# More loads issued in halves, and one more group whose late partitions go HBM to HBM, in a rank-and-scatter kernel

## The chip, the cores and the metric

One core of a Trainium2 chip. The metric is the device time of one launch in microseconds (us), as the median of several runs. All ratios below use runs in the fast state; where a kernel was run once, its state is unknown and I say "one run". The profile is of one further execution; its span runs from the first to the last instruction and is about 2 us under the device time. Where I quote from the trace what no view prints (single DMA packets, single increments of a semaphore), I say so.

## The reference

```python
def reference(x, scores):            # x: 8 x 2048 x 2560 fp32, scores: 8 x 2048 fp32
    order = np.argsort(scores, axis=1)
    ranks = np.argsort(order, axis=1)
    out = np.zeros_like(x)
    out[np.arange(B)[:, None], ranks, :] = x
    return out
```

Each row of x (10,240 bytes) moves to the place that the rank of its score names. 168 MB are read and 168 MB written; the arithmetic is small.

## The kernel before

VectorE counts, for each score, how many of its batch are smaller. The rows are moved in two ways at once:

- Groups of 256 rows are loaded into SBUF by GpSimd (the first group's load by SP, on queue 1) and scattered by two indirect DMAs of 128 rows each (58 such groups, 8 buffers). This is queue 0.
- One group of each of the first six batches, and single rows left out of scatters, go straight from HBM to HBM, one DMA a row, issued by SP (queue 1) and ACT (queue 10). I call these direct rows.

Some loads are issued as two halves. For some groups the scatter leaves out four partitions, by making their rank too large for the bounds check; these 8 rows go as direct rows. In the trace's packet records each of the 14,792 rows scattered is one packet of 10,240 bytes, and each of the 56 left out one of 4 bytes.

```python
THIN = [(b, 4) for b in range(1, B)]        # groups whose scatters skip ...
HOLES = range(48, 48 + 4)                   # ... these partitions
HALVED = range(20)                          # loads issued in two halves
...
def load(line, k, sem):
    ...
    for j in range(m if k in HALVED else 1):
        part = slice(j * D, (j + 1) * D) if k in HALVED else slice(0, m * D)
        line.eng.dma_start(out=xb[k % NBUF][:, part], in_=rows[:, part]).then_inc(sem, 16)
...
# GpSimd, for each group k
if k >= LAG and k + NBUF - LAG < len(BULK):
    scatters_done(pl, k - LAG)              # a buffer comes free
    load_ahead(k + NBUF - LAG)
pl.wait(*loaded[k])
for j in range(GROUPS[g][1]):
    scatter(k, j)                           # bounds_check=N - 1 where (b, g) in THIN
...
nc.gpsimd.drain()
for k in range(max(0, len(BULK) - NBUF), len(BULK)):
    scatters_done(sp, k)                    # SP waits for the last scatters
```

SP waits for all direct rows.

## Time and profile before

| | before |
|---|---|
| device time, median | 778.43 us (778.36 to 778.47) |
| span of the profiled execution | 777.4 us |

The lines are in the prediction.

### The profile page before, as it was taken

To read this page: it belongs to the slowest core of one execution; us is meant where nothing else is said; L and a number is where in the kernel's file an instruction comes from. 1 tells how busy PE (TensorE), PEld (TensorE's weight loads), DVE (VectorE), ACT (ScalarE), POOL (GpSimd) and SP (SyncE) were. 2 spreads that over 40 slices of the span, in tenths; PEclk is the share of its full clock that TensorE was granted. 3 is DMA by queue.
4 is the path that set the end of the run, shared out by engine and by line. 5 is a ranking of instruction groups with operands and counts; after the bars stand their busy time and mean duration, and the time that the engine had idled before them with its cause. 6 is when DMAs were issued, how large, how long until landed. Compare 5 with 4: busy or idle time off the path is not lost.

```text
span 777.4 us, 8189 instructions
## 1 busy us (share of the span) xinstructions
PE 34.6 (4%) x170; PEld 29.9 (4%) x170; DVE 400.0 (51%) x825; ACT 0.0 (0%) x1; POOL 157.4 (20%) x201
## 2 busy tenths in 40 slices
PE   4000010020020020120000000000000000000000
PEld 4000010010010010120000000000000000000000
DVE  5999989979979979889999200000000000000000
ACT  0000000000000000000000000000000000000000
POOL 4114223212112121212121212121211112121000
PEclk9655555555555555565555555555555555555555
DMA  8999999999999999999999999999999999999995
GB/s 358 420 418 420 411 418 414 418 421 415 417 416 419 421 414 424 417 423 416 425 418 423 418 423 418 421 420 422 419 423 419 423 418 423 418 422 419 420 414 188
DMA packets 78914, 320.15 MB, mean 412 GB/s; under 512 B 28640, under 2 KB 54112, under 8 KB 54112
## 3 DMA queue, kind: packets, MB, share of 16 engines
q0 software_dynamic: 27648, 300.90, 91.2%
q1 hardware_dynamic: 25904, 10.93, 5.4%
q10 hardware_dynamic: 25344, 8.16, 4.2%
q14 instruction: 17, 0.14, 0.0%
q8 instruction: 1, 0.02, 0.0%
HBM read 168.41 MB, written 168.35 MB: 433 GB/s over the span
## 4 chain that ended last, share of the span: by engine, by line
DMA 44%; DVE 36%; another core or an unknown queue 5%; issue 4%; PE 3%; POOL 3%; POOLq 0%; SPq 0%
DMA out_dram<-x,rank_i 38%; DVE trash L238 34%; DMA x<-in_x_dram 6%; PE ps_all L196 2%; POOL out_dram L422 2%; DVE s_all L339 2%; POOL x L126 1%; PE ps_row L298 0%; DMA s_in<-in_scores_dram 0%; PE ps_col L175 0%; DVE rank L270 0%; DVE rank_i L276 0%; DVE rank L264 0%; POOLq L446 0%
## 5 line engine op out<-in xcount | busy, mean ns | idle before, releaser
L238 DVE TENSOR_SCALAR_CACHE_REDUCE trash<-s_all,s_col 128x1792 bf16<-128x1792 f32 (+7 forms) x240 | 315.1, 1348 | 4.6
L422 POOL DMA_INDIRECT out_dram<-x,rank_i x116 | 113.0, 974 | 141.5 <-DMA x<-in_x_dram 36.5
L126 POOL DMA_DIRECT2D x<-in_x_dram x76 | 42.6, 563 | 441.8 <-DMA out_dram<-x,rank_i 411.1
L238 DVE SCALAR_TENSOR_TENSOR trash<-s_all,s_col,mask 128x256 bf16<-128x256 f32 x128 | 61.6, 481 | 0.0
L196 PE MATMUL ps_all<-ident,s_col 128*128 128x128 f32 x128 | 27.9, 408 | 3.1 <-DVE s_all L339 2.8
L196 PEld LDWEIGHTS ps_all<-ident,s_col 128*128 128x128 f32 x128 | 26.3, 221 | 4.1 <-DVE s_all L339 3.1
L298 PE MATMUL ps_row<-ident,rank 128*1 128x128 f32 x26 | 6.7, 354 | 392.5 <-DVE rank_i L284 335.2
L339 DVE COPY s_all<-ps_all 128x512 f32<-128x512 f32 x32 | 20.1, 684 | 1.7 <-PE ps_all L196 1.4
L238 DVE DVE_READ_ACCUMULATOR trash<-s_all,s_col 128x1 f32 x240 | 19.7, 82 | 0.0
L298 PEld LDWEIGHTS ps_row<-ident,rank 128*1 128x1 f32 x26 | 1.7, 90 | 395.7 <-DVE rank_i L284 337.4
L238 DVE DVE_READ_ACCUMULATOR trash<-s_all,s_col,mask 128x1 f32 x128 | 10.6, 83 | 0.0
L309 DVE TENSOR_SCALAR thin_i<-ps_row 1x8 int32<-1x8 f32 x7 | 1.1, 154 | 16.7 <-PE ps_row L298 16.7
L324 DVE TENSOR_SCALAR rows_i<-ps_row 1x256 int32<-1x256 f32 x6 | 2.5, 412 | 4.1 <-PE ps_row L298 4.1
L183 DVE COPY s_col<-ps_col 128x128 f32<-128x128 f32 x1 | 0.3, 292 | 4.5 <-PE ps_col L175 4.5
L175 PE MATMUL ps_col<-ident,s_in 8*128 8x8 f32 x16 | 2.1, 264 | 3.7 <-DMA s_in<-in_scores_dram 3.7
L276 DVE CAST rank_i<-rank 128x16 int32<-128x16 f32 (+3 forms) x11 | 2.0, 179 | 0.4
L270 DVE TENSOR_TENSOR rank<-rank,acc 128x16 f32<-128x16 f32 (+3 forms) x11 | 2.0, 178 | 0.4
L175 PEld LDWEIGHTS ps_col<-ident,s_in 8*128 8x128 f32 x16 | 2.0, 211 | 3.7 <-DMA s_in<-in_scores_dram 3.7
L264 DVE TENSOR_TENSOR rank<-acc,acc 128x16 f32<-128x16 f32 (+3 forms) x11 | 1.9, 170 | 0.4
L284 DVE TENSOR_SCALAR rank_i<-rank,hole 128x2 int32<-128x2 f32 x7 | 1.6, 228 | 0.2
L156 POOL TENSOR_SCALAR_AFFINE_SELECT mask<-mask 128x256 f32<-128x256 f32 x2 | 0.8, 402 | 0.0
L168 DVE MEMSET acc<- 128x128 f32 x1 | 0.2, 165 | 1.1 <-SPq L102 1.1
(10 smaller groups left out, 1.8 us busy)
## 6 DMA issues: line engine op xcount, KB each, us to landing
x<-in_x_dram POOLq DMA_DIRECT2D x38, 2560.0 KB
x<-in_x_dram POOLq DMA_DIRECT2D x38, 1280.0 KB
out_dram<-in_x_dram SPq DMA_DIRECT2D x800, 10.0 KB
out_dram<-in_x_dram ACTq DMA_DIRECT2D x792, 10.0 KB
x<-in_x_dram SPq DMA_DIRECT2D x2, 1280.0 KB, 8.6
out_dram<-x,rank_i POOLq DMA_INDIRECT x116, 47.7
s_in<-in_scores_dram SPq DMA_DIRECT2D x1, 64.0 KB
```

Source lines behind the costliest of these rows:

```text
L126: line.eng.dma_start(out=xb[k % NBUF][:, part], in_=rows[:, part]).then_inc(sem, 16)
L175: nc.tensor.transpose(out=ps_col[:, B * c:B * (c + 1)], in_=s_in[:, r + j:r + m * P:m], identity=ident[:B, :B],)
L196: nc.tensor.transpose(out=ps_all[:, P * c:P * (c + 1)], in_=s_col[:, c, b:b + 1].to_broadcast([P, P]), identity=ident[:],)
L238: do(out=trash[i][:, :P * (hi_c - lo_c)], in0=s_all[:, P * lo_c:P * hi_c], accum_out=acc[i][:, col:col + 1], **how,)
L264: nc.vector.tensor_tensor(out=rank[:, cols], in0=acc[0][:, cols], in1=acc[1][:, cols], op=OP.add)
L270: nc.vector.tensor_tensor(out=rank[:, cols], in0=rank[:, cols], in1=acc[2][:, cols], op=OP.add)
L276: nc.vector.tensor_copy(out=rank_i[:, cols], in_=rank[:, cols])
L284: nc.vector.tensor_scalar(out=rank_i[:, cols], in0=rank[:, cols], scalar1=hole[:], scalar2=None, op0=OP.add,)
L298: nc.tensor.transpose(out=ps_row[:1, P * j:P * (j + 1)], in_=rank[:, col:col + 1], identity=ident[:],)
L324: nc.vector.tensor_scalar(out=rows_i[b][:].rearrange("o (p j) -> o p j", p=P), in0=ps_row[:1, :WIDE].rearrange("o (j p) -> o p j", p=P), s ...
L339: nc.vector.tensor_copy(out=s_all[:, 512 * q:512 * (q + 1)], in_=ps_all[:, 512 * q:512 * (q + 1)],)
L422: nc.gpsimd.indirect_dma_start(out=out_flat, out_offset=bass.IndirectOffsetOnAxis(ap=rank_i[:, col:col + 1], axis=0), in_=xb[k % NBUF][:, ...
```

## The change

Two things: the halved loads go from k = 0..19 to k = 0..31, so that queue 0 gives more turns to the direct rows; and group (7, 5) skips partitions 44-47, meant for another late DMA engine, 5.3 us behind the median at the last scatter. By turns I mean packets served: in the trace of the kernel before an engine serves, on average, 41.5 packets of each of the three queues from 480 to 500 us, where loads are whole and direct rows are waiting, and 54.3 of queue 0 from 120 to 140 us, where loads are halved.

```diff
-    THIN = [(b, 4) for b in range(1, B)]
-    HOLES = range(48, 48 + 4)
+    THIN = {**{(b, 4): 48 for b in range(1, B)}, (7, 5): 44}
+    HOLES = sorted(set(THIN.values()))
 
-    HALVED = range(20)
+    HALVED = range(32)
 ...
-    hole = pool.tile([P, 1], F32, name="hole")
+    hole = pool.tile([P, len(HOLES)], F32, name="hole")
 ...   (one mask per hole, and each use picks its own)
-                row = b * N + r + HOLES[i % 4] * m + i // 4
+                row = b * N + r + (THIN[b, g] + i % 4) * m + i // 4
```

More of the change, by code (lines that the diff above doesn't have):

```diff
@@ L209 @@
         bc = broadcast(0)
-        dve.did(
-            nc.vector.tensor_reduce(
-                out=hole[:],
-                in_=ident[:, HOLES[0]:HOLES[0] + 4],
-                axis=mybir.AxisListType.X,
-                op=OP.add,
+        for i, first in enumerate(HOLES):
+            dve.did(
+                nc.vector.tensor_reduce(
+                    out=hole[:, i:i + 1],
+                    in_=ident[:, first:first + 4],
+                    axis=mybir.AxisListType.X,
+                    op=OP.add,
+                )
             )
-        )
         dve.after(dve, dve.n)
@@ L281, in ranks @@
                     cols = slice(b * C + first_col(g), b * C + first_col(g + 1))
+                    i = HOLES.index(THIN[b, g])
                     dve.after(dve, dve.n)
@@ L286, in ranks @@
                             in0=rank[:, cols],
-                            scalar1=hole[:],
+                            scalar1=hole[:, i:i + 1],
                             scalar2=None,
@@ L311, in thin_to_bytes @@
                     in0=ps_row[:1, :P * m].rearrange("o (j p) -> o j p", j=m)[
-                        :, :, HOLES[0]:HOLES[0] + 4
+                        :, :, THIN[b, g]:THIN[b, g] + 4
                     ],
```

## The prediction

> **What bounds the kernel now.** I read the page's slices first, then the queues, the waits, the windows by stage, and last the issues of the final 120 us.
>
> ```profile
> span 777.4 us, 8189 instructions
> ...
> DVE  5999989979979979889999200000000000000000
> ...
> DMA  8999999999999999999999999999999999999995
> GB/s 358 420 418 420 411 418 414 418 421 415 417 416 419 421 414 424 417 423 416 425 418 423 418 423 418 421 420 422 419 423 419 423 418 423 418 422 419 420 414 188
> ...
> q0 software_dynamic: 27648, 300.90, 91.2%
> q1 hardware_dynamic: 25904, 10.93, 5.4%
> q10 hardware_dynamic: 25344, 8.16, 4.2%
> ```
>
> VectorE, which computes the ranks, is done in the 23rd of 40 slices, and the DMA row is at its top digit in all slices but the first and the last. The 16 DMA engines are the bound. Queue 0 (GpSimd's loads and scatters) holds 91.2% of their time; the direct HBM-to-HBM rows of SP (queue 1) and ACT (queue 10) hold 9.6%, and the sum is over 100% because packets of several queues overlap on one engine.
>
> ```profile
> POOL x L126 <- DMA out_dram<-x,rank_i: 411.1, 44, 11.0
> POOL out_dram L422 <- DMA x<-in_x_dram: 36.5, 4, 11.6
> ```
>
> GpSimd, which issues them, waits 411.1 us for buffers to come free: there is room on it for more issues. The chain of waits gives 34% to VectorE's counting, but only because it follows GpSimd's waits back through rows of early batches; the DMA row shows no hole there, so I don't believe that share.
>
> Windows of 40 us (columns: stretch, length, busy time and count of PE, weight loads, VectorE, ACT, GpSimd, then clock, DMA share, GB/s):
>
> ```profile
> 120.00:160.00 40.00, 0.00 (x0) 0.00 (x0) 39.53 (x79) 0.00 (x0) 10.50 (x13) 0.50 1.03 418
> 480.00:520.00 40.00, 0.00 (x0) 0.00 (x0) 0.00 (x0) 0.00 (x0) 7.50 (x9) 0.50 1.02 421
> 760.00:777.40 17.40, 0.00 (x0) 0.00 (x0) 0.00 (x0) 0.00 (x0) 0.00 (x0) 0.50 0.52 161
> ```
>
> The stage with halved loads moves 418 GB/s, that with whole loads 421: halving costs a little. The last 17.4 us are half empty. That is the only stretch with slack, so the change must earn its time there.
>
> ```profile
> 659.49 91.08 ACTq L402 DMA_DIRECT2D out_dram<-in_x_dram  x95
> 660.18 98.17 SPq L402 DMA_DIRECT2D out_dram<-in_x_dram  x102
> ```
>
> ACT issues its last direct row at 750.6 us and SP at 758.4.
>
> From the trace's packet records (start, duration, queue, size) and its semaphore increments I worked out four more things, which no view prints:
> - Durations, as medians: 20,480 B 761 ns, 10,240 B 385 ns, 640 B 32 ns, 4 B (a semaphore write) 9 ns. Two halves take 770 ns and one whole load packet 761: a packet costs 9 ns beside its bytes.
> - The end. Of the 16 increments of the last scatter, 13 come at 765.7 to 766.4 us, the others at 767.9, 771.2 and 772.1. So two engines, call them Y and Z, run 5.3 and 6.1 us behind the median of the 16. The last direct row's increments go on to 775.9 us at steps of 0.19 us.
> - The history of the two. Y's lag grows to about 5 us while VectorE runs, then stands (5.0 at 438 us, 5.3 at 766). Z's grows by some 0.35 us per group all along, and falls by 2 to 3 us at each batch's fifth group, the one whose scatters skip partitions 48-51: 7.2 us at 739, 4.6 at 749, 6.1 at 766. So Z is the engine of partitions 48-51.
> - The direct queues' backlog (rows issued less rows moved, averaged over the engines), SP/ACT: 6/6 at 240 us, where the last halved load has gone out, 24/19 at 400, 35/36 at 560, where it stops growing, 20/11 at 764.
>
> [...] from 480 to 500 us each engine served 41.5 packets of queue 0, 41.5 of queue 1 and 41.5 of queue 10. From 120 to 140 us it served 54.3 of queue 0 but 41 of each other: there the direct rows lacked supply, not turns.
> - [...] 800 rows on queue 1 are 12,800 packets of 640 B, so a direct row is one sixteenth on each engine, while a scattered row sits whole on one.[...]
>
> **The change part by part.**
> 1. Halving 12 more loads (k = 20 to 31). Removes 12 x 128 packets of 20,480 B, adds 12 x 256 of 10,240 B, plus 12 x 16 semaphore writes. Per engine 12 x 8 x 9 ns = 0.86 us and 12 x 9 ns = 0.11 us: +0.97 us on the bounding path. On GpSimd 12 issues of 0.56 us, hidden in its 411 us of waits.
> 2. What halving buys: turns for the direct rows. A row takes two turns of its queue (data, semaphore). A group has per engine 8 load and 16 scatter packets and 3 semaphore writes, 27 turns or 13.5 rows; halved it has 36 turns, 18 rows. The stage from 240 to 397 us (12 groups of 13.1 us) becomes limited by issue, not by turns. Before, SP's queue moved 397 - 233 = 164 rows in it. SP issued 1.09 rows per us over 80 to 240 us and 1.15 over 180 to 240: 157 us of that are 172 to 180. So each queue is ahead by 8 to 16 rows, I take 12. After 397 us it is bound by turns as before, so it stays ahead.
> 3. The skipped partitions of group (7,5). Removes 8 packets of 385 ns from one engine and leaves 8 of 9 ns: -3.0 us on that engine only. Adds 8 direct rows, each 32 + 9 = 41 ns, on every engine: +0.33 us. It is the eighth entry of the list, so ACT takes all 8 rows; ACT then has 800, as SP has.
> 4. VectorE and PE get one more small reduction, one masked rank, one conversion of about 0.15 us, and two transposes. The conversion comes about 330 us before the direct rows' end: nothing.
>
> The end on Z, the engine that comes last. From its last queue-0 packet at 771.2 us to 775.9 it moves direct rows alone; 4.7 us at 0.19 us each are 25 rows, about 17 of SP and 8 of ACT. With 12 moved ahead on each queue and 8 added to ACT: SP 5, ACT 4, so 9 left. Z thus handles 1600 - 9 instead of 1592 - 25 rows under its queue-0 packets, 24 more, at 41 ns: +0.98 us (this holds part 3's +0.33). Its last queue-0 packet ends at 771.2 + 0.97 + 0.98 = 773.2. Then 9 x 0.19 = 1.7 us: 774.9, against 775.9. Net -1.0 us, and part 3's -3.0 us is not in it, because Z is not the engine of 44-47. That relief falls on Y if the author chose well, and Y was already ahead of Z. So 778.4 - 1.0 = 777.4, and a further 0.2 us because unprofiled runs may have a smaller Z lag, where Y's relief counts: 777.2 us. (The last 0.2 is a choice, not a sum.)
>
> **The rivals.**
> - The relief sets the end: Y, not Z, is last in an unprofiled run, or 44-47 are on Z after all. Then up to 3.0 us less, stopped at the next engine. Going from Z at 6.1 to Y at 5.3 allows only 0.8 us on top of the 1.0; should both fall, the engine at 1.9 us would leave up to 4: some 774.5 to 776.5. For it: somebody chose these partitions. Against it: Z's lag falls at the groups that skip 48-51.
> - Halving buys no rows: issue stalls in that stage (SP issued only 16 rows from 60 to 80 us, when every queue had supply), or the backlog fills to the same 35 rows by 740 and throttles again. Then only costs remain: +0.97 + 0.33 = 1.3 us, 779.7 at the worst. Against it: rows moved, not rows waiting, count, and those are ahead.
> - The direct rows finish before the scatters: over 16 rows gained, no rows left alone. Then the last scatter's receipt ends it, 772.1 + 0.97 + 33 x 0.041 = 774.4 instead of 775.9: 776.9.
> - A gain in rate through smaller packets: the windows say the opposite, 418 against 421.
>
> **Range and chances.** The plus and minus terms are each under 3 us in 778, and cancel in part. 8 in 10: 775.5 to 778.8 us. Two per cent are 15.6 us, more than the whole half-empty end after 766 us could give: 0.99 for within 2%, 0.005 for each side.
>
> **What would show it right or wrong.** Queue 0 should have 27648 + 12 x 128 + 12 x 16 = 29376 packets, queue 10 25344 + 8 x 32 = 25600, queue 1 unchanged; loads 62 of 1280 KB and 26 of 2560. The direct backlog should stay near 6 rows to about 397 us and be 9 to 16 rows smaller per queue at 764. The stage from 240 to 400 should fall from about 420 to 418 GB/s. In the last scatter's increments one of the late engines should be 3.0 us nearer the median; if it is Z, my step on who comes last is wrong. If the direct rows are done before the scatters and the time has not fallen, the 0.19 us rows at the end were not what set it.

## More of the kernel before

One view that the prediction did not use is SP's own waits, in columns "who, line <- what it waited for: us in total, times, longest us". Line 28 is the helper of the semaphore waits, line 102 the exit of the program's critical block:

```profile
SPq L28 <- DMA out_dram<-x,rank_i: 13.2, 4, 4.0
SPq L102 <- DMA out_dram<-in_x_dram: 3.8, 1, 3.8
```

After the last scatter SP waited 3.8 us more, for direct rows.

## The result, and the profile after

| | before | after |
|---|---|---|
| device time, median | 778.45 us (778.36 to 778.50, 4 runs) | 775.26 us (774.87 to 775.75, 4 runs) |
| ratio | | 0.9959, 95% interval 0.9942 to 0.9977 |
| span | 777.4 us | 772.8 us |

The change is within 2%, as forecast, but it takes off 3.2 us where I had said 1.2, and 775.26 lies just under my range of 775.5 to 778.8.

The page after, with the lines that answer to those of before:

```profile
span 772.8 us, 8228 instructions
...
DMA  8999999999999999999999999999999999999996
GB/s 358 418 418 420 418 418 418 418 417 418 418 420 417 420 417 417 419 417 419 416 421 421 422 416 426 416 427 417 422 417 424 417 426 415 424 418 424 419 414 283
...
q0 software_dynamic: 29376, 300.82, 91.7%
q1 hardware_dynamic: 25904, 10.93, 5.2%
q10 hardware_dynamic: 25600, 8.24, 4.3%
```

The packet counts are the predicted ones to the unit. The last slice is fuller: 283 GB/s against 188.

The stage in which 12 more loads are halved, before and then after (same columns as in the prediction's windows):

```profile
240.00:400.00 160.00, 12.45 (x58) 10.55 (x58) 149.22 (x307) 0.00 (x0) 30.06 (x36) 0.53 1.02 420
```

```profile
240.00:400.00 160.00, 12.58 (x58) 10.47 (x58) 149.01 (x306) 0.00 (x0) 35.80 (x45) 0.53 1.03 418
```

The stage got slower by the predicted 420 to 418 GB/s, and GpSimd's busy time in it rose by 5.7 us, hidden: over the run it waits 418.5 us for buffers to come free, against 411.1 before. So the gain is not in it. The issues of direct rows at the end, after:

```profile
660.14 74.44 ACTq L404 DMA_DIRECT2D out_dram<-in_x_dram  x78
660.98 75.99 SPq L404 DMA_DIRECT2D out_dram<-in_x_dram  x80
```

SP issues its last direct row at 737.0 us instead of 758.4. And SP's waits, after:

```profile
SPq L28 <- DMA out_dram<-x,rank_i: 33.1, 8, 12.5
SPq L102 <- POOLq L102: 0.9, 1, 0.9
```

The 3.8 us for direct rows after the last scatter are gone. In their place stand 0.9 us in which SP waits for GpSimd's queue. That second line is the clue to what follows.

### The profile page after: what moved, and what is told of

Same layout as the page of the kernel before. It is cut to its first block, busy times and chain, and to the rows that moved or that the text cites. A ratio compares the mean times of both kernels' runs of the same rounds, so it can differ in the third digit from the quotient of the medians.

```text
span 772.8 us, 8228 instructions
## 1 busy us (share of the span) xinstructions
PE 36.2 (5%) x172; PEld 30.4 (4%) x172; DVE 400.7 (52%) x828; ACT 0.0 (0%) x1; POOL 164.6 (21%) x213
## 4 chain that ended last, share of the span: by engine, by line
DMA 63%; DVE 13%; another core or an unknown queue 9%; POOL 6%; issue 4%; PE 1%; POOLq 0%; SPq 0%
DMA out_dram<-x,rank_i 57%; DVE trash L239 12%; DMA x<-in_x_dram 6%; POOL out_dram L424 4%; POOL x L126 2%; PE ps_all L196 0%; DVE s_all L341 0%; DMA s_in<-in_scores_dram 0%; PE ps_col L175 0%; POOLq L448 0%; DVE rank_i L277 0%; DVE rank L271 0%; DVE rank L265 0%; PE ps_row L300 0%
## 5 line engine op out<-in xcount | busy, mean ns | idle before, releaser
L126 POOL DMA_DIRECT2D x<-in_x_dram x88 | 49.4, 565 | 436.9 <-DMA out_dram<-x,rank_i 418.5
L300 PE MATMUL ps_row<-ident,rank 128*1 128x128 f32 x28 | 8.3, 398 | 393.6 <-DVE rank_i L286 386.4
```

What stands on the lines that cost most here:

```text
L300: nc.tensor.transpose(out=ps_row[:1, P * j:P * (j + 1)], in_=rank[:, col:col + 1], identity=ident[:],)
```

## The experiments

Four moments of each trace carry the argument. "Last scatter" is the 16th increment of the last scatter's semaphore, "rows" the last increment of a direct row, "drain" the end of GpSimd's drain instruction; all from the trace's records. "Excess" is the drain's end less the last scatter. The time is the median; runs of one batch share a chip. The moments are those of one profiled execution, which for the kernel before took 779.13 us, 0.7 over its median (778.02 the second time).

| kernel | halved loads | last scatter | rows | drain | excess | time, us | ratio to before |
|---|---|---|---|---|---|---|---|
| before | first 20 | 772.1 | 775.9 | 776.3 | 4.22 | 778.45 | |
| before again | first 20 | 771.2 | 774.8 | 775.4 | 4.22 | 777.86 | 1.0002 |
| after | first 32 | 770.6 | 764.1 | 771.9 | 1.36 | 775.26 | 0.9959 |
| after again | first 32 | 770.7 | 765.8 | 772.1 | 1.36 | 774.99 | 0.9964 |
| halving alone | first 32 | 770.6 | 765.2 | 772.0 | 1.36 | 775.11 | 0.9966 |
| skip alone | first 20 | 770.9 | 775.3 | 775.1 | 4.22 | 778.44 | 1.0013 |
| last 20 halved | last 20 | 772.4 | 756.0 | 776.8 | 4.34 | 778.51 | 1.0009 |
| 26 halved | first 26 | 770.9 | 771.7 | 775.4 | 4.51 | 777.89 | 0.9996 |
| 28 halved | first 28 | 771.2 | 770.8 | 772.5 | 1.32 | 775.17 (1 run) | |

Where the drain ends more than 0.3 us after SP's own waits, the span ends 0.9 us after the drain.

### The two kernels again

Edit: none. Both were run once more, for a second trace.

> The kernel before once more, for a second trace and for the noise. All theories: 778.4 us, within 0.3 us. If the late engines are fixed in place, the last scatter's increments come again 5.3 and 6.1 us behind the median, and the direct rows again end after the scatters (at 776 us).

> The changed kernel once more. All theories: 775.3 us, within 0.5. If its first trace is typical, the direct rows end at 764 us, before the last scatter, and the two late engines stand 2.8 and 4.0 us behind the median at the last scatter. If the smaller Z lag (4.0 against 6.1) was chance, it is back at 6 and the time is nearer 777.

Measured: 777.86 us (ratio 1.0002; on this chip the kernel before is some 0.6 us faster than I had put down) and 774.99 us (0.9964). The late engines came again 4.7 and 6.2 us behind the median in the kernel before, and 2.6 and 4.2 us in the one after. The smaller lag of Z came twice. SP's last waits in the second trace of the kernel before:

```profile
SPq L102 <- DMA out_dram<-in_x_dram: 3.6, 1, 3.6
SPq L102 <- POOLq L102: 0.2, 1, 0.2
```

Here GpSimd came last, after the direct rows, by 0.2 us.

### Each half of the change alone

```diff
 # halving alone                                     # skip alone
-    THIN = {**{(b, 4): 48 ...}, (7, 5): 44}         -    HALVED = range(32)
+    THIN = {(b, 4): 48 for b in range(1, B)}        +    HALVED = range(20)
```

> 12 more halved loads, no skip in group (7,5). Theory A (the rows that the halving moves ahead are the whole gain, the skip gives nothing): 775.0 us, since 8 rows fewer are to move. Theory B (the halving gains until the late engine Y sets the end, and the skip is needed for the rest): Y keeps its 5.4 to 6.0 us lag against 4.0 for Z after the full change, so about 776.7 to 777.3 us. Rival C (the skip is all the gain): 779.4, before plus 1.0 for packets.

> 20 halved loads as before, with the skip in group (7,5). Theories A and B: the direct rows still end last and there are 8 more of them, on ACT, so 778.4 to 778.9 us, no gain though the late engine is 3 us earlier with its scatters. Rival C: 775 to 776 us.

Measured: halving alone 775.11 us (0.9966, 0.9952 to 0.9979), beside 774.99 for both in the same rounds; the skip alone 778.44 (1.0013, 0.9999 to 1.0026). The whole gain is the halving's. Theory A's number, 775.0, came true, but by luck: its reason, the direct rows alone, fell with a later run. The trace says why the skip pays nothing by itself: Y moves up as intended (3.2 us late at the last scatter, where it was 5.3 and 4.7 in the two traces of the kernel before), but Z is still last, 5.6 us late, and the direct rows end later still, at 775.3 us, and set the end:

```profile
SPq L102 <- DMA out_dram<-in_x_dram: 4.3, 1, 4.3
```

In the full change Y is 2.8 and Z 4.0 us late, and Z is last again.

### Is Y the engine of partitions 44-47, and do the late engines set the end?

```diff
 # other partitions                                  # one skip more
-    (7, 5): 44                                      -    (7, 5): 44
+    (7, 5): 60                                      +    (7, 5): 44, (7, 6): 48
```

> The changed kernel with the skip of (7,5) at partitions 60-63 in place of 44-47. If Y is the engine of 44-47, Y stays 4.2 to 5.7 us late instead of 2.7 at the last scatter, the increments show no engine that falls by 3 us at (7,5), and the time is 775.1 to 776.5 us (Y or Z last). If any partition will do, lags as in the changed kernel.

> The changed kernel with one more skip, partitions 48-51 in group (7,6). If Z (4.1 us late at the last scatter) sets the end of the changed kernel, the end moves to Y (2.7 us late): 1.4 us less, 0.3 us of that paid for 8 more direct rows: 774.0 us. If the late engines don't set the end: 775.2 us.

Measured: with partitions 60-63, 776.33 us (0.9983), the two late engines 4.2 and 5.3 us behind, so no late engine was relieved: the run with no such skip, halving alone, had them 4.1 and 4.2 us behind (why the later one is 1.1 us later here is open). With 44-47 skipped the nearer one, Y, stands at 2.8 and 2.6. So partitions 44-47 belong to Y. With one more skip for Z as well: 773.73 us (0.9954; four runs lie within 773.5 to 774.0, the fifth at 775.50), late engines 2.1 and 2.7 us behind, last scatter at 769.6. That is faster than the kernel before and than the change: 1.3 us under the median of the change's second run, in rounds where the kernel before had the same median, 777.72 us. The 95% intervals of the two ratios overlap, but the trace shows 1.0 to 1.2 us at the last scatter, about what was expected. The run with 60-63 shows the same the other way: its last scatter is 1.1 to 1.3 us later than after the change, and its time 1.3 us longer. So once the direct rows are out of the way, and with the drain's excess the same (1.36 us in all of these), the latest engine's last scatter moves the end one for one.

### Does halving pay by giving the direct rows turns?

```diff
-    HALVED = range(20)
+    HALVED = range(38, 58)
```

> The kernel before with the same number of halved loads, 20, but the last 20 (k = 38 to 57) and not the first 20; no skip in (7,5). Theory A (halving pays by giving the direct rows turns so that they end before the scatters; the place matters only through supply): the backlog of direct rows climbs to 35 by about 330 us, falls in the halved stage, is 0 before 760 us, and with no packets added the time is about 1 us under the changed kernel's: 774.2 us. Rival D (halving pays in the middle of the run for another reason, or whole loads late are what is needed): 778 us or more.

Measured: 778.51 us (1.0009). A miss, and the run that overturned my theory. The direct rows behaved as expected: their backlog stood at 30 by 340 us, and they were done at 756 us, 20 us earlier than before. Still nothing was gained. SP's waits in that kernel:

```profile
SPq L28 <- DMA out_dram<-x,rank_i: 20.6, 8, 3.0
SPq L102 <- POOLq L102: 3.9, 1, 3.9
```

Where the kernel before waited 3.8 us for direct rows, this one waits 3.9 us for GpSimd. GpSimd's only work then is its drain, which began at 744 us and ended at 776.8, 4.34 us after the last scatter had landed. Looking back at the kernel before with this in mind: its drain ended at 776.3, and SP was through with the direct rows at 776.1. Two things ended together there, and I had seen one.

### Taking the drain away

```diff
     HALVED = range(38, 58)
 ...
-        nc.gpsimd.drain()
```

No data depends on it, since SP waits for every scatter.

> The last 20 loads halved, as in the run that gained nothing (778.5 us, although its direct rows were done at 756 us), and without GpSimd's drain at the end; SP still waits for every scatter. Theory E (GpSimd's drain, which ended 4.2 to 4.3 us after the last scatter's increments in the kernels with 20 halved loads and 1.4 us after in those with 32, sets the end there): the end comes about 1 to 2 us after the last scatter, so the time falls by 2.5 to 3.5 us to 775 to 776. Theory F (the 4.3 us are needed by something else on GpSimd, or by the end of any kernel with so many issues): 778.5 us again.

Measured: 783.73 us (1.0075), slower, and correct. GpSimd runs a drain anyway at the program's end; it now began at 772.4 us, when all data had landed, and took 8.6 us. Theory E is right that the drain sets the end and wrong that it can be dropped: the drain at the end takes time even with no DMA in flight. The kernel's own drain, begun 28 us before the last scatter landed, left only 4.34 us after it; that it does part of its work beside the last scatters would fit, and is not shown.

### What makes the drain short?

```diff
 # 12 tiny DMAs more                                 # one DMA of 108 elements an engine more
+  for i in range(12):                               +  nc.gpsimd.dma_start(
+      nc.gpsimd.dma_start(                          +      out=extra[:],
+          out=extra[:, i:i + 1],                    +      in_=x[0, 0:16, 0:216:2],
+          in_=scores[0:1, 16*i:16*(i+1)]            +  )
+              .rearrange("o p -> p o"))
```

(Both on the kernel before, right after the first loads, here without their semaphores; SP waits for them at the end.)

> The kernel before with 12 more, tiny DMAs of 64 bytes issued by GpSimd at the start: 204 DMAs of GpSimd as in the changed kernel, but only 24 more packets on each engine and not 108. If the drain's length depends on the number of DMAs that GpSimd issued, it ends 1.4 us after the last scatter; if on descriptors, it stays above 4 us. Time in both cases 777.5 to 778.5 us, because the direct rows still end at about 775 us.

> The kernel before with one more DMA of GpSimd, of 108 elements of 4 bytes for each engine: 193 DMAs, but 1728 + 109 = 1837 packets of queue 0 on each engine, as the changed kernel has 1836. If the drain's end after the last scatter depends on the packets queued so far, it is about 1.4 us; if on the DMAs, about 4.3 us. The direct rows still end at about 775 us, so the time stays at 777 to 778.5 us.

Measured: 779.58 us (1.0016, over the 777.5 to 778.5 that I had expected) and 778.44 us (one run). The drain ended 3.65 us after the last scatter in both, to the hundredth. With 204 DMAs of GpSimd it is not short, so the number of DMAs does not make it short. The second kernel's 108 elements went as two packets an engine (256 and 176 bytes), 1731 packets in all and not the 1837 that I had put down: that run excludes the number of elements moved, not the number of packets.

```diff
-    HALVED = range(32)                              # old skips throughout
+    HALVED = range(26)      # and 28, 30, 58, range(26, 58)
```

> 26 halved loads, old skips: half the dose. The direct rows are some 10 rows a queue further than before, so about 15 of the 30 are left at 764 us and end some 2 to 3 us earlier, near 773 us. Theory A with the rows alone: 776.5 us. With the drain: 198 DMAs; a drain that is still 4.2 us long after the last scatter at 771.5 ends at 775.7, so 777.2 us; a short one leaves 776.0 us.

> 28 halved loads, old skips: 200 DMAs of GpSimd, 1800 packets an engine. The direct rows end near 769 us, before the last scatter. If the drain is short as soon as the direct rows end before the scatters: 1.4 us after, 775 us in all. If its length is a matter of counts, it goes on rising from the 4.5 us of 26 halved loads until some count where it falls, or has fallen already.

> 30 halved loads, old skips: 202 DMAs, 1818 packets an engine. As for 28; one of the two should show between which counts the drain falls from 4.5 to 1.4 us. With 1.4: 775 us; with 4.6: 778 us.

> All 58 loads halved, old skips: 230 DMAs, 2070 packets an engine. 26 halvings more than the changed kernel cost 26 x 81 ns = 2.1 us and buy nothing. If the drain rises by 4 to 5 ns a packet after its fall, it ends about 2.4 us after the last scatter: 778 us. If it stays at 1.4: 777 us; if it falls once more, in between.

> The last 32 loads halved instead of the first 20, old skips. Direct rows done before 764 us. 205 DMAs of GpSimd, 1845 packets of queue 0 on an engine: if the drain's length depends on either, it ends about 1.4 us after the last scatter, and the time is set by Z, 5.8 us late as with the last 20 halved: about 776 us. If halving late is itself what makes the drain long, it stays at 4.3 us and the time is 779.

Measured:

- 26 halved: 777.89 us (0.9996). Direct rows done at 771.7 us, 3 to 4 us earlier than before, and nothing gained: excess 4.51.
- 28 and 30 halved: 775.17 and 774.66 us (one run each), excess 1.32 in both.
- 58 halved: 776.94 us (one run), excess 2.71. Between 32 and 58 the halvings cost, as far as one run shows.
- Last 32 halved: 776.51 us (0.9979), excess 1.69; direct rows done at 732 us. Z is 5.2 us late, so its last scatter, at 772.3, is later than after the change.

Between 26 and 28 halved loads the time falls by 2.7 us and the excess by 3.2. SP's waits of the kernel with 26, then of that with 28:

```profile
SPq L102 <- POOLq L102: 3.4, 1, 3.4
SPq L102 <- DMA out_dram<-in_x_dram: 0.7, 1, 0.7
```

```profile
SPq L102 <- POOLq L102: 0.9, 1, 0.9
```

With 26 halved, 0.7 us are still for direct rows and 3.4 for GpSimd. One difference was left between these two besides the number of halved loads: with 26 the direct rows end after the last scatter, with 28 before. The next two runs turn that order round with the number held.

```diff
 # 26 halved, fewer direct rows                      # 28 halved, more direct rows
-    {(b, 4): 48 for b in range(1, B)}               -    {(b, 4): 48 ...}
+    {(b, 4): 48 for b in range(2, B)}               +    {**{(b, 4): 48 ...}, (7, 6): 60, (7, 7): 60}
```

> 26 halved loads as in the run with the long drain (its direct rows ended at 771.7 us, after the last scatter at 770.9), but without the skip of batch 1: 8 direct rows fewer on SP, and 3 us more scatters on Z. The direct rows then end about 770 us, some 3 us before the last scatter at 773 to 774. If the drain is long because the direct rows end after the scatters: now 1.3 us, time 777.5. If it is a matter of the number of halved loads or packets: still 4.5 us, time 780.

> 28 halved loads as in the run with the short drain (direct rows ended at 770.8 us, before the last scatter at 771.2), with two more skips, of partitions 60-63 in (7,6) and (7,7): 8 direct rows more on SP and on ACT, so SP's end at about 772.5 us, after the last scatter at 771.6. If direct rows that end last make the drain long: 4.5 us after the last scatter, 778.5 us. If it is a matter of halved loads or packets: 1.3 us, and SP's direct rows or the drain end it at 773: 775.7 us.

Measured: 779.83 us (1.0016) and 776.50 us (0.9975). With 26 halved the direct rows now ended at 764.8, 8 us before the last scatter, and the excess stayed 4.51. With 28 they ended at 773.5, after the last scatter at 772.0, and the excess stayed 1.32. The order of ends does not matter to the drain. SP's waits, with 26 and then with 28:

```profile
SPq L102 <- POOLq L102: 4.1, 1, 4.1
```

```profile
SPq L102 <- DMA out_dram<-in_x_dram: 1.4, 1, 1.4
```

The second of these also shows the other leg: with a short drain, late direct rows set the end.

So the drain's excess goes with the number of halved loads: 4.2 to 4.5 us at 20 and 26, 1.3 to 2.7 at 28 and above, in 17 of 17 traces where it began before the last scatter landed, with 3.65 in the two with extra DMAs. Kernels with the same loads have the same excess within 0.01 us (4.22 in three traces, 1.36 in five), whatever their late engines and direct rows did. By what it goes with them stays open. It is not the number of DMAs, and it does not slide with the direct rows. Packets queued on an engine would fit as a bound (1782 and fewer: long, 1800 and more: short), but no run crossed it without changing loads, and below it the number alone does not order the excess: 4.22 us at 1728 packets, 3.65 at 1731, 4.34 at 1737, 3.65 at 1752.

### What the direct rows cost an engine, and why Z is late

```diff
-    THIN = {...}                                    -    DIRECT = range(6)
+    THIN = {}                                       +    DIRECT = range(0)
```

> All groups through load and scatter, no direct rows and no skips; the result stays correct. About 790 to 795 us by packets (64 groups x 16 x 385 ns of scatters and 392 us of loads on each engine). If Z's steady lag comes from the direct rows, it doesn't grow here. If it is of its own loads and scatters, it grows by 0.3 us per group as before, to some 20 us. The period of a group without direct rows, against 13.1 us with 27 rows, gives what one direct row costs an engine: 41 ns by packet durations, about 30 if packets of different queues overlap.

Measured: 799.05 us (one run, slower than the 790 to 795 expected), correct. A window of it (columns as before but without ACT), where VectorE is done and no direct row moves:

```profile
480.00:520.00 40.00, 0.00 (x0) 0.00 (x0) 0.00 (x0) 8.07 (x10) 0.50 1.01 431
```

431 GB/s, against 421 in the same window of the kernel before: direct rows use the engines less well. A group takes 12.18 us here and 13.11 there with 27 direct rows in it, so a row costs an engine 0.93 / 27 = 34 ns, under the 41 ns of its two packets. From 454 to 710 us the three latest engines stand 3.7, 4.7 and 7.2 us behind the mean of the first twelve at every scatter, without any drift. So Z's steady drift comes with the direct rows and not from its own loads and scatters.

The packet records show how. From 440 to 740 us of the kernel before, 151 of 5904 scatter packets take more than 405 ns where the median is 385; without direct rows none of 6333 does. No two of the 151 run at the same time, where 151 picked at random would overlap some 40 times, so they look like one engine's. What the scatter packets take over 385 ns adds up to 0.3 to 0.4 us a group, and Z drifts by 0.35. That the engine is Z follows from this fit alone, for the records carry no engine number.

## Why the prediction was right or wrong

**What held.** The counts of packets and issues; the cost of halving (418 against 421 GB/s); that GpSimd's extra issues are hidden; that VectorE's part does not matter (it is done in the 23rd of 40 slices, as before); that Y is helped by the skip and Z by partitions 48-51 (its lag falls from 7.2 to 4.6 us at such a group, before), though Y by less than the 3.0 us said; that the change stays within 2%. That direct rows get more turns from smaller packets also held, and one could read it off: where loads are whole, the backlog grows (before, on SP's queue, from 6 rows at 240 us to 35 at 560), and where they are halved, it stands at some 3 to 6 rows (after the change up to 400 us).

**The step that failed** is the first sentence of "The end on Z": "From its last queue-0 packet at 771.2 us to 775.9 it moves direct rows alone", which I then took for what sets the end, and the sum "9 x 0.19 = 1.7 us: 774.9, against 775.9". The end had two legs, direct rows at 776.1 and GpSimd's drain at 776.3. The drain did not figure in the prediction at all, though the kernel calls it two lines above its end. The run with the last 20 loads halved removed the first leg alone and gained nothing; 26 halved loads shortened it by 3 to 4 us and gained nothing. The change paid because its 12 halvings also took the drain's excess from 4.22 to 1.36 us. Over the two traces of each kernel the span fell by 3.9 us on average (777.4 and 776.3 to 772.8 and 773.0): 2.9 us of it are the drain's excess and 1.0 us is the earlier last scatter. (The medians of the device times fell by 2.9 to 3.2 us; the first profiled execution of the kernel before was one of its slower ones.) The first leg had to go too: SP was through with the direct rows only at 776.1, and the run with 28 halved loads and more direct rows shows that these set the end once the drain is short.

**Sizes that were off,** by the prediction's own terms:

- "I take 12" rows moved ahead on each queue. At 740 us SP's queue had moved 769 rows against 748 and ACT's 773 against 749: 21 and 24. SP issued 1.15 rows per us from 240 to 400 us, the upper rate of the two that I had, and the queue moved nearly all of them, 182 rows against 164; the rest of the lead came before 240 us, where both kernels are the same, and so is a matter of the run. With 21 rows the direct rows end before the scatters. That was my third rival ("the direct rows finish before the scatters"), and as an order of events it was the one that came; its time, 776.9 us, was not, for it had no drain either.
- "+0.97 + 0.98" later for Z's last packet, 773.2 us. It came at 770.1 and 770.3. Of this, the median engine's last scatter came only 1.1 us later than before (766.0 and 765.0 before, 766.6 twice after, where runs of one kernel differ by 1.0). The rest is Z: its lag to the median was 6.1 and 6.2 us before and 4.0 and 4.2 after (5.3 with partitions 60-63), about 2 us that no term of mine held. Before, Z's lag grew to the end; after, it stood from about 746 us on. In the tail of the kernel before, the trace shows scatter packets of Z starting every 462 ns on average (430 to 490) and those of Y every 415, with direct rows between them, and every 381 ns after the change, where there are none left. Z's packets themselves take some 420 ns there, Y's the usual 385. That direct rows slow Z more than the others is shown by this and by the run without any; how that adds up to 2 us I have not worked out, and why Z suffers more stays open.
- The "-3.0 us on that engine only": at the last scatter Y came 1.3 to 1.5 us nearer the median by the skip alone (4.1 us with the halving alone, 2.8 and 2.6 with both), so about half.
- The "further 0.2 us" for Y's relief: nothing, as halving alone was as fast as both.

## What to carry to other kernels

When several things wait at a program's end, list every one with its end time before naming the bound: here direct rows and a drain ended within 0.2 us of each other, and moving the direct rows alone gained nothing. A gain that comes out larger than its mechanism allows deserves the same search as one that is missing: run each part alone, then move the supposed cause without the change. In a kernel that keeps all DMA engines full, look at the latest engine of the last transfer, not at the mean; relieving the two latest ones (773.73 us against 774.99) gained more than the skip of the change (774.99 against 775.11).
